# The order of M1 and M2 units in the first chunk of a decoder's MLP

## The chip, the cores and the metric

The kernel runs on one core of a Trainium2 chip. The metric is device time in microseconds (us) of one execution; lower is better.

## What is computed

The reference is a decoder of two layers with 512 tokens and a model width of 1024, in float32. The change lies in the first layer's MLP:

```python
def sq_relu_mlp(h, w1, w2):
    return jnp.square(jax.nn.relu(h @ w1)) @ w2
...
        h = modulate(rmsnorm(x, norm_mlp_g[i]), sh2, sc2)
        x = x + g2[:, None, :] * sq_relu_mlp(h, mlp_w1[i], mlp_w2[i])
```

`w1` is 1024 by 4096 and `w2` 4096 by 1024. Below, M1 is the product with `w1` and M2 the product with `w2`.

## The kernel before

**Precision.** Each float32 operand is split into a high part, rounded to the matmul's input type, and a low part, the rest. A product is three matmuls (function `mm3`, lines 187, 188 and 190): low weight times high operand, high times low, high times high. A weight tile `raw`, `b` or `bt` is split by `split`: ScalarE copies it to `wh` (line 176), then VectorE subtracts to give `wl` (line 177). `parts` does the same to activations (lines 638 and 639). The `wh` and `wl` tiles have five places each.

**The MLP's units.** The 4096 hidden features are worked in four chunks, each of two groups of four 128-feature blocks. The function `mlp` makes a list of units and runs them in order on TensorE, whose order is written out by hand; the compiler orders the other engines. There are four kinds:

- `f`: one 128-feature block of M1 in the plain way (chunk 0 only; the last of them is the first unit of the list).
- `s`, written `(c, j, m)`: one of the seven block products by which M1 for chunk c, group j is formed (a scheme with seven products in place of eight). It has 24 matmuls, each 256 columns wide. Products 1, 6, 7 and 4 accumulate in one PSUM bank and 5, 3 in another, 2 in a third: `start` is set only for m = 1, 5, 2. After products 1, 6 and 5, ScalarE copies the bank to the tile `g` (line 828); after 2, 3 and 7, VectorE combines the bank with `g` (lines 831, 833 and 835); then ScalarE applies relu and square (lines 836 and 667). The next product on a bank may write it only after that read.
- `p`, written `(c, m)`: one of the seven products of M2 for chunk c, 24 matmuls 512 columns wide over two token halves. Products 1, 6, 7 and 4 share one pair of banks, 5 and 3 another. Each is added to `y` on VectorE (line 930; the first time on ScalarE, line 933).
- `q`: the last chunk of M2, in the plain way.

**The weights of a unit.** M1's sums of weight blocks are formed in place. For m = 5 and 6, VectorE adds a block (line 788); after the split of m = 5 and of m = 6, GpSimd issues an accumulating DMA that adds another block for a later product (line 783). Product 4 of a group so uses the tile that product 6 has split, after such a transfer. Plain loads are issued by SyncE (line 159). They share three buffers, and a load waits for a buffer until the last split from it is done. M2's products 1, 5, 6 and 4 go through one tile `bt` in the same way: after each split GpSimd issues the accumulating transfer for the next of them (line 850).

**Preparation ahead.** At each unit n the loop first emits the preparations (loads, sums, splits) of the units from n on that fit a budget: an `s` counts 1, a `p` counts 2, and at most 5 are counted (`ahead`). Then come the extra jobs whose number is n (a modulation column: one-element copy on ScalarE, line 214, and a 128x1024 multiply with accumulation on VectorE, line 215; one column is due at unit 8), and then the run of unit n on TensorE with the reads of its bank.

**The order of units.** For layer 0, chunk 0 the list begins with the rest of `f`; then `lead` units of kind `s`; then, after each `p` in `ORDER2` = (1, 2, 5, 6, 3, 7, 4), as many `s` units as `step` says. The `s` units are those of chunk 1: group 0 in the order 1, 2, 5, 6, 3, 7, 4 and then group 1 in the order 1, 5, 6, 3, 7, 2, 4.

Of the kernel before, what the change touches and what calls it, by code (L numbers as in the profile page):

```python
# [81 lines left out]
def decoder_kernel(ctx: ExitStack, tc: tile.TileContext, xtok, vecs, rows, fgrow, ada0, adag, ada1, pool_w, w1s, w1, w1f, w1b, w2, w2e, w_v, w_u, w_o, wsT, lnp, bs, out):  # L82
# [561 lines left out]
    def mlp(i, first, extra, last, ending):  # L644
# [3 lines left out]
        with (  # L648
# [328 lines left out]
            for c in range(3):  # L977

                early = i == 0 and c == 0
                fs = [("s", (c + 1, j, m)) for j in range(2) for m in (ORDER2 if early and j == 0 else ORDER)]  # L980
                lead, step = (3, (0, 3, 2, 2, 2, 2, 0)) if early else (2, (1, 2, 3, 2, 2, 2, 0))
                units += fs[0:lead]
                fs = fs[lead:]
                for m, n in zip(ORDER2, step):
                    units.append(("p", (c, m)))
                    units += fs[0:n]
                    fs = fs[n:]
# [118 lines left out]
    ex += [(59, lambda: spread_cols(mods[0][:, c_g(1, 0) : c_g(1, 0) + KD], "gain0"))]  # L1106
    ex += [(n, modulation(q, get4)) for q, n in enumerate(COLUMNS) if q >= 19]
    mlp(0, first0, ex, gated, ending0)


# [6 lines left out]
    with (  # L1117
# [79 lines left out]
        for dh in range(2):  # L1197
            wo = blocks(w_o[dh])

            early = 6 if dh == 0 else KD  # L1200
# [60 lines left out]
    ex = [x for q in range(8) for x in modulation_late(48 + q, 8 + 5 * q, late_gb if q == 0 else get_gb)]  # L1261
    ex += [(58, lambda: spread_cols(mods[1][:, c_g(1, 0) : c_g(1, 0) + KD], "gain1"))]
    mlp(1, first1, ex, last1, lambda: None)


# [78 lines left out]
```

## Time and profile before

| what | value |
|---|---|
| three runs | 854.56, 855.83, 855.63 us |
| median | 855.63 us |
| the profiled execution | 853.81 us |
| its span, from first to last instruction | 852.1 us |
| mean granted TensorE clock | 0.993 of full speed |
| moved by DMA | 186.53 MB, 219 GB/s on the mean |

The engines are TensorE (PE; its weight loads are PEld), VectorE (DVE), ScalarE (ACT), GpSimd (POOL) and SyncE (SP). A letter q behind the name is an engine's instruction queue, where DMA issues stand. In a timeline row, the bracket at the end gives the time that the engine stood idle before the instruction and what released it. A matmul's shown length overlaps that of the next: the step from start to start is what one takes from TensorE's time.

The changed stretch lies from about 97 us, when the last `f` unit begins, to 184 us, when chunk 1 begins.

### The profile page before, as it was taken

The page shows a single profiled execution, that of the slowest core. Times are in us where ns is not written, and L with a number is a line of the kernel's source. Part 1 is how long each engine was busy: PE and PEld are TensorE (multiplying, and loading weights), DVE is VectorE, ACT ScalarE, POOL GpSimd, SP SyncE. Part 2 cuts the span into 40 slices and gives each one's busy share as a digit, 9 for nine tenths or more (in the row PEclk, how much of TensorE's full clock was granted, in tenths as well). Part 3 has the DMA queues.
Part 4 walks back from the last instruction along what each step waited for, and adds up shares of the span by engine and source line. Part 5 has one row for each costly group of instructions (what it writes and reads, how often), then busy time and mean ns, then how long its engine had stood idle before and what let it go on. Part 6 is the DMA issues. An engine that isn't in the chain of part 4 may idle for free.

```text
span 852.1 us, 13021 instructions
## 1 busy us (share of the span) xinstructions
PE 837.4 (98%) x5068; PEld 744.6 (87%) x5068; DVE 695.8 (82%) x928; ACT 490.9 (58%) x728; POOL 70.3 (8%) x95
## 2 busy tenths in 40 slices
PE   9999999999999999999999999999999999999996
PEld 7778898998998998888888888999999999999885
DVE  6889798978997998867897865777788888987755
ACT  5286776765756567247233226666766666566521
POOL 3000011010101010000020001010101000111001
PEclk9999999999999999999999999999999999999998
DMA  8969998988888896724745636947888788777302
GB/s 349 418 234 323 357 216 217 288 212 236 211 282 195 274 237 205 272 98 173 256 166 176 218 123 224 320 94 202 208 238 221 207 222 241 182 168 243 125 25 99
DMA packets 44082, 186.53 MB, mean 219 GB/s; under 512 B 4955, under 2 KB 5107, under 8 KB 36726
## 3 DMA queue, kind: packets, MB, share of 16 engines
q1 hardware_dynamic: 35282, 137.72, 43.7%
q0 software_dynamic: 8304, 45.63, 26.7%
q10 hardware_dynamic: 436, 2.37, 0.8%
q8 instruction: 40, 0.66, 0.3%
q14 instruction: 20, 0.16, 0.1%
HBM read 179.39 MB, written 6.30 MB: 218 GB/s over the span
## 4 chain that ended last, share of the span: by engine, by line
PE 87%; DMA 6%; ACT 3%; DVE 2%; issue 1%; SPq 0%; POOLq 0%; POOL 0%; DVEq 0%; ACTq 0%
PE po L187 16%; PE po L188 16%; PE po L190 16%; PE pm L188 12%; PE pm L190 12%; PE pm L187 12%; DMA wh<-in_ada 2%; DMA bt<-in_w 2%; DMA wl<-in_ada 1%; DMA ada<-in_adag 1%; PE po L1182 1%; ACT sq L315 1%; PE px L1062 1%; ACT wh L176 0%; PE po L611 0%
## 5 line engine op out<-in xcount | busy, mean ns | idle before, releaser
L187 PE MATMUL po<-hb,wl 128*128 128x256 f32 (+2 forms) x633 | 187.9, 297 | 2.3 <-ACT g L828 2.1
L188 PE MATMUL po<-hb,wh 128*128 128x256 f32 (+1 forms) x632 | 187.2, 296 | 0.0
L190 PE MATMUL po<-hb,wh 128*128 128x256 f32 (+1 forms) x632 | 187.1, 296 | 0.0
L177 DVE TENSOR_TENSOR wl<-raw,wh 128x1024 fp32r<-128x1024 f32 (+1 forms) x128 | 152.8, 1198 | 39.4 <-ACT wh L176 36.8
L176 ACT ACTIVATE wh<-raw 128x1024 fp32r<-128x1024 f32 (+1 forms) x128 | 131.9, 1038 | 79.6 <-PE pm L190 26.7
L190 PE MATMUL pm<-wh,oh 128*128 128x512 f32 (+1 forms) x375 | 131.1, 367 | 0.0
L187 PE MATMUL pm<-wh,ol 128*128 128x512 f32 x336 | 131.0, 390 | 0.0
L188 PE MATMUL pm<-wl,oh 128*128 128x512 f32 x336 | 131.0, 390 | 0.0
L187 PEld LDWEIGHTS po<-hb,wl 128*128 128x128 f32 x633 | 119.6, 189 | 7.0 <-ACT g L828 2.3
L190 PEld LDWEIGHTS po<-hb,wh 128*128 128x128 f32 x632 | 119.5, 189 | 4.1
L188 PEld LDWEIGHTS po<-hb,wh 128*128 128x128 f32 x632 | 119.4, 189 | 3.9
L190 PEld LDWEIGHTS pm<-wh,oh 128*128 128x128 f32 x375 | 70.4, 188 | 14.7
L187 PE MATMUL po<-as,wl 128*128 128x256 f32 x288 | 79.9, 277 | 0.7 <-DVE wl L177 0.7
L188 PE MATMUL po<-as,wh 128*128 128x256 f32 x288 | 79.6, 277 | 0.0
L190 PE MATMUL po<-as,wh 128*128 128x256 f32 x288 | 79.6, 276 | 0.0
L177 DVE TENSOR_TENSOR wl<-bt,wh 128x1024 fp32r<-128x1024 f32 x48 | 58.4, 1222 | 23.5 <-ACT wh L176 23.5
L215 DVE SCALAR_TENSOR_TENSOR ada<-ada,cb 128x1024 f32<-128x1024 f32 x56 | 68.1, 1219 | 10.4 <-DMA ada<-in_ada 7.8
L187 PEld LDWEIGHTS pm<-wh,ol 128*128 128x128 f32 x336 | 63.1, 188 | 11.9
L188 PEld LDWEIGHTS pm<-wl,oh 128*128 128x128 f32 x336 | 63.1, 188 | 11.7
L176 ACT ACTIVATE wh<-bt 128x1024 fp32r<-128x1024 f32 x48 | 50.3, 1057 | 25.6 <-DMA bt<-in_w 15.9
L187 PEld LDWEIGHTS po<-as,wl 128*128 128x128 f32 x288 | 54.1, 188 | 0.9 <-ACT wh L176 0.9
L188 PEld LDWEIGHTS po<-as,wh 128*128 128x128 f32 x288 | 54.2, 188 | 0.0
(218 smaller groups left out, 1549.9 us busy)
## 6 DMA issues: line engine op xcount, KB each, us to landing
ada<-in_ada SPq DMA_DIRECT2D x72, 512.0 KB, 4.5
raw<-in_w1b SPq DMA_DIRECT2D x48, 512.0 KB, 5.5
b<-in_w SPq DMA_DIRECT2D x18, 1024.0 KB, 6.8
bt<-in_w POOLq DMA_DIRECT2D x18, 1024.0 KB, 8.0
raw<-in_w1b POOLq DMA_DIRECT2D x24, 512.0 KB, 5.7
raw<-in_w2e SPq DMA_DIRECT2D x16, 512.0 KB, 4.3
bt<-in_w SPq DMA_DIRECT2D x6, 1024.0 KB, 9.8
b<-in_w POOLq DMA_DIRECT2D x6, 1024.0 KB, 11.1
```

What stands on the lines that cost most here:

```text
L176: A.activation(h[:, c], r[:, c], AF.Copy)
L177: V.tensor_tensor(l[:, c], r[:, c], f32(h[:, c]), ALU.subtract)
L187: T.matmul(o[:, c], wl, mh[:, c], start=first and not c.start, stop=False, **kw)
L188: T.matmul(o, wh, ml, start=False, stop=False, **kw)
L190: T.matmul(o[:, c], wh, mh[:, c], start=False, stop=last and c.stop is None, **kw)
L215: V.scalar_tensor_tensor(r, r, 1.0, cb, ALU.mult, ALU.mult, accum_out=pmv[i, b][:, j : j + 1])
L315: A.activation(j, X(t)[:, c], AF.Square, scale=D**-0.5, accum_out=out)
L1062: T.transpose(px[:, 256 * q + P * r : 256 * q + P * r + P], xs[r][:, P * (k + q) : P * (k + q) + P], ident)
L1182: T.matmul(po[:, tok[t]], vt[t][:, ch, c0 : c0 + P], wb[:, 0, hd], start=True, stop=True)
```

## The change

One tuple: after product 2 of M2, four `s` units in place of three, and after product 7 one in place of two.

```diff
-                lead, step = (3, (0, 3, 2, 2, 2, 2, 0)) if early else (2, (1, 2, 3, 2, 2, 2, 0))
+                lead, step = (3, (0, 4, 2, 2, 2, 1, 0)) if early else (2, (1, 2, 3, 2, 2, 2, 0))
```

The units with their numbers, S standing for `s` of group 0, T for `s` of group 1, P for `p` of chunk 0:

| n | 5 | 6 | 7 | 8 | 9 | 10 | 11 | 12 | 13 | 14 | 15 | 16 | 17 | 18 | 19 | 20 | 21 |
|---|---|---|---|---|---|---|---|---|---|---|---|---|---|---|---|---|---|
| before | P2 | S6 | S3 | S7 | P5 | S4 | T1 | P6 | T5 | T6 | P3 | T3 | T7 | P7 | T2 | T4 | P4 |
| after | P2 | S6 | S3 | S7 | S4 | P5 | T1 | T5 | P6 | T6 | T3 | P3 | T7 | T2 | P7 | T4 | P4 |

So four M2 units (P5, P6, P3 and P7) each change places with the `s` unit behind them. Units 0 to 8 and 20 onwards keep their numbers, as do the extra jobs. By the budget of `ahead`, the preparations move with them: in the code, P5's goes from unit 6 to unit 7, S4's from 7 to 6, T5's from 10 to 9, P6's from 10 to 11, P3's from 13 to 14, T3's from 13 to 12, P7's from 16 to 17, T2's from 16 to 15, and P4's stays at 19.

## The prediction

> **What bounds the kernel now.** I read the page's shares first, then the list of what TensorE waits for from 98 us to 380 us, then TensorE's timeline around the changed stretch, then ScalarE's and VectorE's timelines of the same microseconds. S1 to S7 are the M1 units of `(1, 0, m)`, T1 to T7 those of `(1, 1, m)`, P1 to P7 the M2 units of chunk 0.
>
> ```profile
> span 852.1 us, 13021 instructions
> PE 837.4 (98%) x5068; PEld 744.6 (87%) x5068; DVE 695.8 (82%) x928; ACT 490.9 (58%) x728; POOL 70.3 (8%) x95
> PE 87%; DMA 6%; ACT 3%; DVE 2%; issue 1%; SPq 0%; POOLq 0%; POOL 0%; DVEq 0%; ACTq 0%
> ```
>
> TensorE is busy 98% of the span and makes 87% of the chain that ended last. So an edit that only reorders TensorE's units (same matmuls, same number) can change the time only through TensorE's idle stretches, and the slow clock behind them. In the stretch of the change there is exactly one:
>
> ```profile
> PE po L187 <- ACT g L828: 2.1, 1, 2.1
> PE po L187 <- DVE wl L177: 0.7, 1, 0.7
> ```
>
> The 2.1 lies here, the 0.7 in chunk 1, at 272 us (last row):
>
> ```profile
> 127.87 0.28 PE L190 MATMUL po<-as,wh 128*128 128x256 f32 x1
> 130.25 0.38 PE L187 MATMUL po<-hb,wl 128*128 128x256 f32 x1 [2.10 <-ACT g L828]
> ...
> 134.58 0.28 PE L190 MATMUL po<-hb,wh 128*128 128x256 f32 x1
> 134.69 0.39 PE L187 MATMUL pm<-wh,ol 128*128 128x512 f32 x1
> ...
> 140.15 0.29 PE L187 MATMUL po<-hb,wl 128*128 128x256 f32 x1
> ...
> 142.89 0.28 PE L187 MATMUL po<-hb,wl 128*128 128x256 f32 x1
> ...
> 145.61 0.39 PE L187 MATMUL pm<-wh,ol 128*128 128x512 f32 x1
> ...
> 272.18 0.36 PE L187 MATMUL po<-as,wl 128*128 128x256 f32 x1 [0.72 <-DVE wl L177]
> ```
>
> Columns: start and length in us, engine, line, operation, tiles, idle time before it and its releaser. The last matmul of S3 starts at 127.87. S7 cannot begin, because it accumulates on the bank that S6's copy (line 828) has still to read. S7 runs from 130.25 to 134.69, P5 to 140.15, S4 to 142.89, T1 to 145.61. S4 and T1 take 5.46 us together, 2.73 each, and P5 takes 5.46. S7 took 4.44, 1.71 more than its sisters. The table by stretch (PE, PEld, DVE, ACT and POOL busy, granted clock, DMA share, GB/s) says why:
>
> ```profile
> 120.00:128.00 8.00, 8.00 (x61) 7.53 (x59) 6.77 (x7) 3.00 (x4) 0.86 (x1) 1.00 1.00 275
> 128.00:130.00 2.00, 0.15 (x2) 0.00 (x0) 1.20 (x2) 2.00 (x3) 0.00 (x0) 1.00 1.04 274
> 130.00:132.00 2.00, 1.75 (x9) 1.76 (x10) 1.16 (x2) 0.47 (x2) 0.55 (x1) 0.63 1.02 385
> 132.00:134.00 2.00, 2.00 (x12) 2.00 (x11) 1.19 (x2) 1.62 (x2) 0.30 (x1) 0.51 1.04 254
> 272.00:274.00 2.00, 1.82 (x16) 1.85 (x17) 2.00 (x4) 2.00 (x3) 0.87 (x1) 1.00 0.84 166
> ```
>
> After the stop of 2.27 us (127.98, one issue step of 0.11 behind 127.87, to 130.25) the granted clock is 0.63 and 0.51; after the one of 0.7 us it stays 1.00. The present stall therefore costs 2.27 + 1.71 = 3.98 us, all that this stretch could give back. The DMA engines are full throughout (share 1.00 to 1.04).
>
> **Why S7 waits, and what stands behind it.** ScalarE, then VectorE, then the descriptor issues of GpSimd and SyncE:
>
> ```profile
> 127.70 2.00 ACT L176 ACTIVATE wh<-bt 128x1024 fp32r<-128x1024 f32 x2 [5.00 <-DMA bt<-in_w]
> 129.62 0.58 ACT L828 ACTIVATE g<-po 128x512 f32<-128x512 f32 x1
> 131.72 1.06 ACT L176 ACTIVATE wh<-raw 128x1024 fp32r<-128x1024 f32 x1 [1.53 <-DMA raw<-in_w1b]
> 133.16 1.06 ACT L176 ACTIVATE wh<-raw 128x1024 fp32r<-128x1024 f32 x1 [0.38 <-DMA raw<-in_w1b]
> 134.25 0.20 ACT L214 ACTIVATE pmv<-wh 128x1 f32<-128x1 f32 x1
> ```
> ```profile
> 132.81 1.23 DVE L177 TENSOR_TENSOR wl<-raw,wh 128x1024 fp32r<-128x1024 f32 x1 [1.65 <-ACT wh L176]
> 133.95 0.69 DVE L833 TENSOR_TENSOR g<-po,g 128x512 f32<-128x512 f32 x1
> 134.55 1.22 DVE L177 TENSOR_TENSOR wl<-raw,wh 128x1024 fp32r<-128x1024 f32 x1
> 135.69 1.22 DVE L215 SCALAR_TENSOR_TENSOR ada<-ada,cb 128x1024 f32<-128x1024 f32 x1
> 136.83 0.68 DVE L835 TENSOR_TENSOR g<-g,po 128x512 f32<-128x512 f32 x1
> ...
> 174.13 1.28 DVE L930 TENSOR_TENSOR y<-y,pm 128x512 f32<-128x512 f32 x2
> ```
> ```profile
> 111.65 0.85 POOL L850 DMA_DIRECT2D bt<-in_w  x1 [0.63 <-DVE wl L177]
> 122.46 0.86 POOL L783 DMA_DIRECT2D raw<-in_w1b  x1 [9.96 <-DVE wl L177]
> 131.45 0.85 POOL L850 DMA_DIRECT2D bt<-in_w  x1 [8.13 <-DVE wl L177]
> ```
>
> P5's two splits stood in ScalarE's queue ahead of S6's copy, and waited until 127.70 for the accumulating transfer issued at 111.65. Next come S4's split (131.72, waiting for its transfer issued at 122.46), T1's (133.16, waiting too) and the one-element copy of line 214. VectorE follows in the order of the code: S4's low part, the combination of S3 (833), T1's low part, the modulation column placed at unit 8 (215), and only then S7's combination (835), done at 136.83 + 0.68 = 137.51.
>
> **The change, part by part.** TensorE goes from S6 S3 S7 P5 S4 T1 P6 T5 T6 P3 T3 T7 P7 T2 T4 P4 to S6 S3 S7 S4 P5 T1 T5 P6 T6 T3 P3 T7 T2 P7 T4 P4. No instruction is added or removed.
>
> *P5 behind S4.* Its preparation moves in the code from unit 6 to unit 7, behind S6's copy; S4's moves ahead from 7 to 6. That can free S7, and is worth 3.98 us at most. The price is that P5's 5.46 us no longer lie between S7 and S4. They cover two things today. First, S4 continues S7's accumulation on the same bank (start only at m = 1, 5, 2), and may not write it before line 835 has read it. Second, S4's weights arrive late: split from 131.72, low part done at 132.81 + 1.23 = 134.04. Both are over by 137.51, 2.64 us ahead of S4's start at 140.15; directly behind S7 they aren't.
>
> When does 835 end then? Everything ahead of it on VectorE stays ahead of it in the code: P5's splits (unit 7 rather than 6), S4's low part (6), 833 (unit 7's run), T1's low part and the column (unit 8), and 835 is unit 8's run. T1's low part hangs on a transfer that lands at 133.1. So I leave 835's end at 137.51, whether S7 runs early or late, and S4 starts 0.05 behind it (as S7 did: 129.62 + 0.58 = 130.20, start 130.25), at 137.56. TensorE has then stood for 2.87 us (from 134.69, S7 still late) or 6.85 (from 127.98 + 2.73 = 130.71, S7 on time). Both are longer than the 2.27 that dropped the clock, so S4 takes 4.44. Sum: 137.56 + 4.44 + 5.46 (P5) = 147.46, against 142.89 where T1 starts now: **+4.57 us**. The bounds of this term: if 835 costs no queueing at all, S4 starts at its own data (134.05), which gives 134.05 + 4.44 + 5.46 = 143.95, +1.06; if S4's data came too, the gain of the last rival below.
>
> In a sentence by itself: the Trainium skill ("TensorE: Matmul & The Clock Gate", "What's actually happening") says that the clock drops after at least one idle window of some 3.4 us, by which 2.87 us of idling could leave S4 at full speed and the sum would be 137.56 + 2.73 + 5.46 - 142.89 = +2.86. The trace disagrees: 2.27 us of idling were followed by a clock of 0.63 and 0.51.
>
> The other three units, with two more rows of TensorE (T5's and T2's first matmul):
>
> ```profile
> 151.07 0.29 PE L187 MATMUL po<-as,wl 128*128 128x256 f32 x1
> ...
> 172.91 0.29 PE L187 MATMUL po<-hb,wl 128*128 128x256 f32 x1
> ```
>
> *P6 behind T5, P3 behind T3.* P6's accumulating issue at 131.45 hangs on P5's split, not on its run, and P6's first matmul (145.61 now) comes 4.57 + 2.73 later, so its transfer gains cover. T5 and T3 each come 5.46 earlier against the M2 unit that they pass. T5 would start at 147.46 + 2.73 = 150.19; it starts at 151.07 now with no wait before it. I take nothing; as nearest row for a loss I take the 0.7 us wait for a low part, below nothing I exclude, since no idle time is left there to win. The orders of the accumulating issues on POOL and of the loads on SP stay (S4's, then P5's; T5's and T6's splits still trigger theirs).
>
> *P7 behind T2.* P4 adds on P7's banks and needs both line-930 adds out of them. P7 ends at 172.91 now, the two adds at 174.13 + 1.28 = 175.41, 2.50 behind it. T4 alone, 2.73, now covers that in place of T2 and T4's 5.46. I take nothing, with 0.23 to spare; another VectorE operation of 1.22 ahead of the adds would cost 1.0.
>
> From T1 on TensorE has no idle time in which a delay could be made up, so +4.57 goes to the end. The profiled execution took 853.81 us (span 852.1 and 1.7 around it), 1.82 below the median of the runs, 855.63. The profiled one becomes 858.4, the median **860.2**.
>
> **The rivals.** One more row, of the page's transfers (the last number is the median of us from issue to landing):
>
> ```profile
> raw<-in_w1b POOLq DMA_DIRECT2D x24, 512.0 KB, 5.7
> ```
>
> *S4's split also goes ahead of S6's copy on ScalarE.* For it: S4's preparation moves to unit 6, ahead of the run of S6. Against: its transfer is issued 10.8 us after P5's, and the compiler places work when it believes it ready. Then the copy follows at 132.78 to 133.3, S7 runs 133.35 to 137.8, P5's splits push T1's to 137.3, and low part, column and 835 end near 140.2. S4 from there, slow, and P5 end at 150.1: +7.2, 862.8.
>
> *835 slips ahead of T1's low part and the column.* For it: the compiler does reorder VectorE when it believes an operand ready. Against: here the rows run in the order of the code. With S7 on time, 835 follows 833 at 134.6 to 135.3, S4 at 135.3, +2.3; with S7 late, 835 ends at 135.5, the stop of 0.9 keeps the clock, S4 at 135.55: +0.9. So 856.5 to 857.9.
>
> *Faster.* S6's copy goes first, S7 runs 127.98 to 130.71, and S4's transfer lands in time. It takes 131.7 - 122.5 = 9.2 us now. The page's median for transfers of this kind is 5.7. With that S4's raw lands at 128.2 and its low part ends near 130.5; 835 alone stands between S7 and S4, some 0.8 us, too short to drop the clock: 3.98 - 0.8 = 3.2 gained, 852.4. It decides from S4's start: to gain anything, this must come before 142.89 - 5.46 - 2.73 = 134.70 with the clock kept, and before 132.99 with the clock dropped, and 835 must stand at the head of VectorE's queue as well. Against it: a DMA share of 1.00 to 1.04 until 134 us, with the same transfers ahead, which makes S4's data end at 134.04.
>
> *The clock holds* through S4's stop of 2.87. The rows show it kept after 0.72 and dropped after 2.27, once each, and a single drop may have had its moment by chance. S4 then takes 2.73: 137.56 + 2.73 + 5.46 = 145.75, +2.86, 858.5. Against it stands the 0.51. (The window of the Trainium skill's page is a reason for it.)
>
> **How the numbers follow.** Forecast 0.50; S4's split ahead of the copy 0.12; 835 early 0.18; faster 0.14; clock holds 0.06. What a measurement here tells from no change is about 0.2%, 1.71 us. Faster beyond that: most of the faster case, 0.11. Within: half of 835 early and the rest of the faster case, 0.12. Slower: 0.50 + 0.12 + 0.09 + 0.06 = 0.77. The range begins at 855.0, where most of the faster case is left out, and ends at 863.4, the second case plus half of the 1.0 at P7; outside lies some 0.15.
>
> **What would show it.** Right: in the profile after, S4's first matmul shows an idle time of 2.5 us or more released by VectorE's line 835, with the clock near 0.5 for 3 us behind it, and 835 stands behind T1's low part and line 215. S7's wait for line 828 may be gone or not; it doesn't change the sum. Wrong: S4 waits for line 177 (its own data decide), or for under 1 us; or TensorE stops in front of P4; or S7 waits longer than now.

## The result, and the profile after

| kernel | runs | median, us | lowest to highest |
|---|---|---|---|
| before | 6 | 855.25 | 853.51 to 857.06 |
| changed | 6 | 863.29 | 859.18 to 865.73 |

The ratio is 1.0092, with a 95% interval of 1.0065 to 1.0119: the changed kernel is slower by 8.0 us. The profiled execution is the slowest of its six (865.73 us), so its stretches are read against each other rather than its span.

The shares of the page and the list of TensorE's waits after the change:

```profile
span 863.7 us, 13019 instructions
PE 845.0 (98%) x5068; PEld 750.5 (87%) x5068; DVE 696.8 (81%) x928; ACT 492.0 (57%) x728; POOL 69.8 (8%) x95
PE 75%; DVE 9%; DMA 8%; ACT 4%; issue 4%; POOLq 0%; DVEq 0%; POOL 0%; ACTq 0%
```
```profile
PE po L187 <- ACT g L828: 4.7, 1, 4.7
PE po L187 <- DVE g L835: 3.0, 1, 3.0
...
PE pm L187 <- DVE y L930: 0.6, 1, 0.6
```

TensorE's part of the chain that ended last fell from 87% to 75%, and VectorE's rose from 2% to 9%. The forecast let the stall on S6's copy (line 828) go or stay; it more than doubled. A second one, on S7's combination (line 835), came new, as forecast. TensorE's rows there are S7's, S4's, P5's and T1's first matmul:

```profile
133.31 0.57 PE L187 MATMUL po<-hb,wl 128*128 128x256 f32 x1 [4.71 <-ACT g L828]
...
140.96 0.58 PE L187 MATMUL po<-hb,wl 128*128 128x256 f32 x1 [3.04 <-DVE g L835]
...
146.25 0.63 PE L187 MATMUL pm<-wh,ol 128*128 128x512 f32 x1
...
152.09 0.29 PE L187 MATMUL po<-hb,wl 128*128 128x256 f32 x1
```

T1 starts at 152.09 in place of 142.89, 9.20 later. S6 began at 122.98 in place of 122.53 here, so the stretch from S6 to T1 takes 29.11 us in place of 20.36, 8.75 more. Why S7 waited so long stands in ScalarE's rows, and why S4 did in VectorE's:

```profile
122.13 1.04 ACT L638 ACTIVATE oh<-s 128x1024 fp32r<-128x1024 f32 x1
131.71 1.06 ACT L176 ACTIVATE wh<-raw 128x1024 fp32r<-128x1024 f32 x1 [8.54 <-DMA raw<-in_w1b]
132.67 0.58 ACT L828 ACTIVATE g<-po 128x512 f32<-128x512 f32 x1
133.15 1.99 ACT L176 ACTIVATE wh<-bt 128x1024 fp32r<-128x1024 f32 x2
135.05 1.04 ACT L176 ACTIVATE wh<-raw 128x1024 fp32r<-128x1024 f32 x1
```
```profile
132.80 1.23 DVE L177 TENSOR_TENSOR wl<-raw,wh 128x1024 fp32r<-128x1024 f32 x1 [5.56 <-ACT wh L176]
133.94 1.22 DVE L869 TENSOR_TENSOR s<-s,g 128x1024 f32<-128x1024 f32 x1
135.07 2.35 DVE L177 TENSOR_TENSOR wl<-bt,wh 128x1024 fp32r<-128x1024 f32 x2
137.34 0.69 DVE L833 TENSOR_TENSOR g<-po,g 128x512 f32<-128x512 f32 x1
137.94 1.22 DVE L177 TENSOR_TENSOR wl<-raw,wh 128x1024 fp32r<-128x1024 f32 x1
139.08 1.22 DVE L215 SCALAR_TENSOR_TENSOR ada<-ada,cb 128x1024 f32<-128x1024 f32 x1
...
140.22 0.68 DVE L835 TENSOR_TENSOR g<-g,po 128x512 f32<-128x512 f32 x1
```

ScalarE took S4's split first and stood 8.54 us for its transfer, with S6's copy behind it; P5's two splits, whose data had landed by 127.70 in the kernel before, followed the copy. On VectorE, P5's low parts then stood behind S4's and ahead of 833, T1's low part, the column and 835, and so did line 869, which forms P6's operand. In the kernel before, P5's low parts had run ahead of S4's, and line 869 behind 835:

```profile
128.80 2.36 DVE L177 TENSOR_TENSOR wl<-bt,wh 128x1024 fp32r<-128x1024 f32 x2 [2.02 <-ACT wh L176]
...
137.50 1.22 DVE L869 TENSOR_TENSOR s<-s,g 128x1024 f32<-128x1024 f32 x1
```

S4's low part started when it had started before (132.80 and 132.81), and from there VectorE worked without a gap. From start to start, line 869 took 1.13 us and P5's two low parts 2.27. Their sum is what 835's end moved, from 137.51 to 140.90. The granted clock (the third number from the end, after five engines' busy times; then DMA share and GB/s) dropped behind both stops:

```profile
134.00:136.00 2.00, 2.00 (x11) 2.00 (x11) 2.00 (x3) 2.00 (x4) 0.00 (x0) 0.50 0.46 143
136.00:138.00 2.00, 1.91 (x14) 1.72 (x12) 2.00 (x4) 1.13 (x3) 0.28 (x1) 0.81 0.30 119
...
140.00:142.00 2.00, 1.04 (x5) 1.04 (x6) 2.00 (x5) 1.03 (x2) 0.00 (x0) 0.54 1.02 205
142.00:144.00 2.00, 2.00 (x11) 2.00 (x11) 1.95 (x3) 1.26 (x2) 0.86 (x1) 0.50 0.94 197
...
146.00:148.00 2.00, 2.00 (x10) 1.67 (x9) 0.00 (x0) 1.51 (x3) 0.00 (x0) 0.75 1.02 209
```

### The profile page after: what moved, and what is told of

It is laid out like the page before. It is cut to its first block, busy times and chain, and to the rows that moved or that the text cites. A ratio compares the mean times of both kernels' runs of the same rounds, so it can differ in the third digit from the quotient of the medians.

```text
span 863.7 us, 13019 instructions
## 1 busy us (share of the span) xinstructions
PE 845.0 (98%) x5068; PEld 750.5 (87%) x5068; DVE 696.8 (81%) x928; ACT 492.0 (57%) x728; POOL 69.8 (8%) x95
## 4 chain that ended last, share of the span: by engine, by line
PE 75%; DVE 9%; DMA 8%; ACT 4%; issue 4%; POOLq 0%; DVEq 0%; POOL 0%; ACTq 0%
PE po L187 13%; PE po L190 13%; PE po L188 13%; PE pm L187 9%; PE pm L188 9%; PE pm L190 9%; DVE wl L177 4%; DMA raw<-in_w1b 4%; DMA ada<-in_ada 3%; PE po L479 2%; PE pg L431 1%; ACT wh L176 1%; DVE ada L215 1%; DMA bt<-in_w 1%; DVE y L930 1%
## 5 line engine op out<-in xcount | busy, mean ns | idle before, releaser
L187 PE MATMUL po<-hb,wl 128*128 128x256 f32 (+2 forms) x633 | 189.8, 300 | 7.9 <-ACT g L828 4.7
L188 PEld LDWEIGHTS po<-hb,wh 128*128 128x128 f32 x632 | 121.1, 192 | 3.9
L190 PEld LDWEIGHTS po<-hb,wh 128*128 128x128 f32 x632 | 120.5, 191 | 4.1
```

The costliest lines, as they stand in the source:

```text
L187: T.matmul(o[:, c], wl, mh[:, c], start=first and not c.start, stop=False, **kw)
L188: T.matmul(o, wh, ml, start=False, stop=False, **kw)
L190: T.matmul(o[:, c], wh, mh[:, c], start=False, stop=last and c.stop is None, **kw)
```

## The experiments

Ratios are to the kernel before, run on the same chip with each.

**Which of the four swaps costs.** The change taken apart: P5 behind S4 alone, and the other three units alone.

```diff
-(0, 3, 2, 2, 2, 2, 0)
+(0, 4, 1, 2, 2, 2, 0)    p5_alone
+(0, 3, 3, 2, 2, 1, 0)    others_alone
```

> Only P5 and S4 change places; T5, T6, T3, T7, T2 stand as before against P6, P3 and P7. Theory A (the loss sits in front of S7 and S4, from P5's move alone): 863.3, within 1.5, with two idle times of TensorE of about 4.7 and 3.0 us, released by lines 828 and 835. Rival C (a part of the loss comes from the other three units): clearly under 863, down to 860 if half of it lies there.

> P5 stays ahead of S4; P6, P3 and P7 move behind T5, T3 and T2. Theory A: no change, 855.3 within 1.7, with S7's idle time of 2.1 us on line 828 as before and no new one in chunk 0. Rival C: 857 to 859, with a new idle time in front of P4 or one of the moved units.

`p5_alone` took 863.61 us, ratio 1.0092 (1.0069 to 1.0115), as much as the whole change, with the same two waits:

```profile
PE po L187 <- ACT g L828: 4.6, 1, 4.6
PE po L187 <- DVE g L835: 3.0, 1, 3.0
```

`others_alone` took 856.45 us, ratio 1.0029 (1.0012 to 1.0045): a miss for "no change". S7's wait was 0.7 us there, not the expected 2.1, and P4 waited for P7's adds. TensorE's row comes first, then VectorE's:

```profile
177.78 0.47 PE L187 MATMUL pm<-wh,ol 128*128 128x512 f32 x1 [1.41 <-DVE y L930]
```
```profile
175.81 1.23 DVE L177 TENSOR_TENSOR wl<-raw,wh 128x1024 fp32r<-128x1024 f32 x1 [1.18 <-ACT wh L176]
176.95 1.27 DVE L930 TENSOR_TENSOR y<-y,pm 128x512 f32<-128x512 f32 x2
```

A low part stood ahead of the adds and waited for ScalarE. To see whether P7 makes that price, P6 and P3 were moved without it, by `(0, 3, 3, 2, 1, 2, 0)`.

> P6 and P3 move behind T5 and T3, P5 and P7 stay as before. In the run others_alone (856.45 against 854.06) P4 waited 1.4 us for the line-930 adds of P7. Theory G (that wait is the price of the three units, as P7's shorter cover): no wait in front of P4, 854.1 within 1.0. Rival C' (T5 and T3 ahead of P6 and P3 cost it): 856.4 again.

It took 856.17 us, ratio 1.0004 (0.998 to 1.0028), with no wait in front of P4. S7, in the same place in both runs, waited 0.7 us there and 2.9 here. The missing wait at P4 fits P7's shorter cover as the price, but the two intervals overlap, so it isn't shown. In the profile of the whole change P4 doesn't wait, so this price isn't always paid there.

**The state that the forecast had assumed.** The changed order on TensorE, with S4's preparation behind P5's, so that ScalarE and VectorE keep the order of before as far as T1's split.

```diff
-                for m in range(n, ahead(n)):
+                for m in {6: (6, 7, 8), 7: (7, 8, 10, 9)}.get(n if i == 0 else None, range(n, ahead(n))):
```

> TensorE's order of the changed kernel, but S4's preparation is put behind P5's at unit 7, so that ScalarE and VectorE keep the order of the kernel before up to T1's split. This is the state that the forecast assumed. The forecast's step: S7 waits 2.1 us on line 828 as before, 835 ends at 137.5 and S4 starts there: 855.25 + 4.6 = 859.8. Theory A (S4's split ahead of the copy on ScalarE adds the rest): the same 859.8, and so 3.4 of the 8.0 us come from that queue. Rival D (P5's missing cover alone costs all of it, whatever ScalarE's order): 863.3.

It took 859.84 us, ratio 1.0063 (1.0038 to 1.0087). S4 started at 137.58, where the forecast had put it (137.56), and the release is the forecast's. S7's wait was 1.2 us rather than 2.1:

```profile
129.68 0.38 PE L187 MATMUL po<-hb,wl 128*128 128x256 f32 x1 [1.20 <-ACT g L828]
...
137.58 0.58 PE L187 MATMUL po<-hb,wl 128*128 128x256 f32 x1 [4.81 <-DVE g L835]
...
142.87 0.44 PE L187 MATMUL pm<-wh,ol 128*128 128x512 f32 x1
```

`p5_alone`, run beside it, has a median 3.8 us higher. So about that much of the loss goes with ScalarE's order and what it does to VectorE's; the two intervals overlap, so the size is rough. The edit put P5's low parts back ahead of S4's and line 869 back behind 835 (138.65) at once, and can't part those two. Rival D's 863.3 lies outside the interval.

**Does S7's start matter?** The same kernel, with S6's copy on VectorE, where it goes ahead of P5's low parts.

```diff
-                    A.activation(t, po, AF.Copy)
+                    V.tensor_copy(t, po) if (i, c, j, m) == (0, 1, 0, 6) else A.activation(t, po, AF.Copy)
```

> The kernel of the run after_s4_behind with S6's copy on VectorE, ahead of P5's low parts, so that S7 doesn't wait at all. The forecast said that whether S7 runs early or late doesn't change the sum. Theory A: S7 starts at 128 us, TensorE then stands for 6.8 us until line 835 ends, S4 starts at 137.5 as in after_s4_behind, and the time is 1.0063 of the kernel before, within 0.0025. Rival I (an earlier S7 is worth something): 1.0045 or less, with S4 at 135.5 or earlier.

It took 859.9 us, ratio 1.007 (1.0042 to 1.0097). S7 started on time, at 128.22; S4 waited 6.45 us and began at the same moment as in `after_s4_behind`:

```profile
137.56 0.58 PE L187 MATMUL po<-hb,wl 128*128 128x256 f32 x1 [6.45 <-DVE g L835]
```

So in this order 835 decides when S4 starts, and S7's start doesn't.

**What decides 835.** First VectorE's queue: T1's preparation and the column one unit later, on top of `after_s4_behind`.

```diff
+... 8: (8, 9, 10)} ...
-COLUMNS = (0, 5, 8, 11, ...
+COLUMNS = (0, 5, 9, 11, ...
```

> The kernel of the run after_s4_behind, and T1's preparation at unit 9 and the modulation column due at unit 9 in place of 8, so that line 835 (S7's combination) no longer stands behind T1's low part or line 215 on VectorE. Theory A (S4 waits for 835, and 835 for what is queued ahead of it): 835 ends some 1.2 to 2.3 us earlier, S4 starts at 135.3 to 136.4 in place of 137.6, and the time is 857.5 to 858.7 against 859.84. Rival E (VectorE is full here, and what moves behind 835 is missed in front of P5 or T5): 859.8 again, with a new idle time there.

It took 857.77 us, ratio 1.0035 (1.0014 to 1.0056). VectorE's rows show that only the column moved behind 835; T1's low part still stood ahead of it:

```profile
134.04 1.22 DVE L177 TENSOR_TENSOR wl<-raw,wh 128x1024 fp32r<-128x1024 f32 x1
135.17 0.68 DVE L835 TENSOR_TENSOR g<-g,po 128x512 f32<-128x512 f32 x1
```

S4 started at 135.91, 1.67 earlier than in `after_s4_behind`. The column makes 1.13 of that; the rest is that S4's low part began at 132.30 in place of 132.83, with its transfer landing earlier. No new wait appeared in front of P5 or T5. The median is 2.1 us below that of `after_s4_behind`, as expected, but the two ran on different chips, and the intervals of their ratios overlap. Rival E's 859.8 against 854.06 would be 1.0067, outside this run's interval. The next run takes the transfer away. It leaves one block out of S4's weight sum, so it only probes the time:

```diff
-                if m == 6:
+                if m == 6 and (i, c, j) != (0, 1, 0):
                     add(t, *CHAIN[4])
```

> The changed kernel without the accumulating transfer into S4's weights (product 4 of chunk 1, group 0, layer 0 is computed with its weight sum one block short). S4's split waits for nothing then. Theory A (both stops of the changed kernel come from that transfer's landing at 131.7, by ScalarE's queue): S7's wait shrinks from 4.7 to about 1.2 us (P5's first split still stands ahead of the copy), 835 ends at 135.5 to 137.5 behind T1's split, and the time is 856.8 to 858.8 against 854.1 before. Rival F (all the loss is that transfer's): 854 or less. Rival D (P5's missing cover): 862 to 863.

It took 855.87 us, ratio 1.0014 (0.9995 to 1.0033): less than theory A had asked. S7 didn't wait; T1's transfer, with 512 KB less on the way, landed at 129.19, in place of 133.16 in the kernel before; and 835 let S4 go at 134.18:

```profile
129.19 1.06 ACT L176 ACTIVATE wh<-raw 128x1024 fp32r<-128x1024 f32 x1 [0.93 <-DMA raw<-in_w1b]
```
```profile
134.18 0.58 PE L187 MATMUL po<-hb,wl 128*128 128x256 f32 x1 [2.84 <-DVE g L835]
```

From S6 to T1 it took 22.30 us, against 20.36 before and 29.11 after the change. So most of the loss hangs on what lands when, by S4's transfer itself and by its share of full DMA engines; the run can't part these two. The missing cover still costs: S4 stood 2.84 us and then took 5.28, and the stall of S7 that is gone here pays for only a part of that.

**What the old stall was worth.** The kernel before, with S6's copy on VectorE and P5's preparation at unit 7.

```diff
-                for m in range(n, ahead(n)):
+                for m in range(n, 9 if (i, n) == (0, 6) else ahead(n)):
```

> The kernel before with S6's copy on VectorE, ahead of P5's low parts there, so that S7 no longer hangs on ScalarE's wait for P5's transfer. If the stall in front of S7 is worth the 2.27 us and the slow clock behind it: 855.25 - 3.9 = 851.3, no idle time in front of S7 and a clock of 1.00 from 128 to 136 us. Rival: the next late item takes its place (P5's own low part, ready at 131.1 against 130.7): P5 waits 0.4 us, 851.7. If the stall was worth only its idle time: 853.0.

It took 856.15 us, ratio 1.0012 (0.9997 to 1.0028). That is a miss: nothing was gained. The wait on line 828 is gone from TensorE's list, the clock stays 1.00, and others stand in its place:

```profile
PE pm L187 <- DVE ol L639: 1.3, 1, 1.3
PE pm L187 <- DVE y L930: 1.2, 1, 1.2
...
PE po L187 <- DVE g L835: 1.0, 1, 1.0
```

S4 can't start before 835 in the old order either (137.50 here), P6 waits for its operand at 144.73, and in chunk 1 a unit waits for line-930 adds. With 835 ahead of the column a part of it comes:

```diff
-                for m in range(n, 9 if (i, n) == (0, 6) else ahead(n)):
+                for m in range(n, {6: 9, 8: 11}.get(n if i == 0 else None, ahead(n))):
-COLUMNS = (0, 5, 8, 11, ...
+COLUMNS = (0, 5, 9, 11, ...
```

> The kernel of the run before_copy_vector, and T1's preparation and the modulation column at unit 9. There S4 waited 1.0 us for line 835, and P6 1.3 us for the low part of its operand. Theory H (S7's stop is only the first of several things that end at the same time, set by the transfers): S4's wait goes, P6's stays or grows by the same, 853 to 855.5 against 854.06. Rival (the first stop is all that counted): 851.0 to 852.

It took 853.3 us, ratio 0.9976 (0.9958 to 0.9995). The same kernel ran once more:

> The kernel of the run before_read_early again, beside the one with the operand formed early: 0.9976 of the kernel before, between 0.9955 and 0.9995. Theory H: no wait for S7 and S4, one of about 1 us in front of P6.

It took 853.12 us, ratio 0.9978 (0.9963 to 0.9993). In this run S7 and S4 wait no longer; P6 does, and a unit in chunk 1:

```profile
142.84 0.50 PE L187 MATMUL pm<-wh,ol 128*128 128x512 f32 x1 [0.71 <-DVE ol L639]
...
206.71 0.47 PE L187 MATMUL pm<-wh,ol 128*128 128x512 f32 x1 [0.78 <-DVE y L930]
```

This is the one version here that is faster than the kernel before, by some 2 us. Going after P6's wait as well, by forming its operand early (line 869 behind P5's operand split), gained nothing further:

```diff
                 parts((oh, ol), a)
+                if (i, c, m) == (0, 0, 5):
+                    V.tensor_tensor(a, a, quad(c, 0, 0), ALU.subtract)
```

> The kernel of the run before_read_early, in which only P6 still waited (0.95 us for the low part of its operand), with the subtraction that forms this operand (line 869) emitted behind P5's operand split rather than at P6's preparation. Theory H: P6's wait goes or gives way to one for P6's weights, ready 0.2 to 0.4 us before that low part: 0.2 to 0.9 us below the run before_read_early_2 of the same call.

It took 854.23 us, ratio 0.9993 (0.9973 to 1.0012), 1.1 us more than `before_read_early_2` beside it. P6 then waited 0.6 and 0.8 us for its weights, and the wait in chunk 1 grew to 1.4.

## Why the prediction was right, and where not

**The direction and its cause were right.** Without P5 between them, S4 waits for 835, and 835 for VectorE's queue. The signs that the forecast had named for this came: TensorE stood 3.04 us in front of S4 for line 835, which had T1's low part and line 215 ahead of it, and the clock was 0.54 and 0.50 behind the stop. Where ScalarE kept the old order, S4's start (137.58 and 137.56, forecast 137.56) and release came out as worked out. P5's swap alone gave the ratio of the whole change (1.0092).

**The size was wrong, and the range held by luck.** The forecast was +4.57, the medians moved by 8.0. The 863.29 lies inside the stated range by 0.1 us only, and the range reached that far because the first rival's 862.8 and half of a price at P7 set its end. One of the forecast's own signs of being wrong came too: S7 waited longer than before (4.71 against 2.10). In the profile the parts add up: 4.57 as forecast, 3.40 for S4's later start (140.96 against 137.56) and 1.23 more for the clock, less the 0.45 by which S6 began later, make the 8.75.

**The step that failed** is "I leave 835's end at 137.51, whether S7 runs early or late", on the ground that "Everything ahead of it on VectorE stays ahead of it in the code". That S7's start doesn't matter held (`after_s7_on_time`). But 835 ended at 140.90. S4's split ran ahead of S6's copy on ScalarE, as its preparation now stands in the code, and waited until 131.71 for its transfer. So P5's splits came at 133.15 in place of 127.70, and P5's low parts (2.27) behind S4's on VectorE, not ahead of it. And line 869 (1.13), which the forecast's list doesn't have, came ahead of 835; what it costs by itself is open, as no run moves it alone. T1's split, at 135.05 in place of 133.16, added nothing here: it was done at 136.09, before VectorE came to T1's low part at 137.94. With the old order back on both engines (`after_s4_behind`), 835 ended at 137.53.

This was the first rival, given 0.12 against 0.50 for the forecast. The evidence put against it, that S4's transfer is issued 10.8 us after P5's, tells when the data land and not in which order the compiler queues the work. The rival had the copy and S7's start right (132.67 and 133.31, against 132.78 and 133.35). It had 835 end near 140.2 because T1's split was to be pushed to 137.3, which didn't happen; other work, P5's low parts and line 869, took about as long. So that its +7.2 comes close to the 8.0 is in part luck.

**The clock's term** had a price that one profile can't fix. S4 was given 4.44 us at the dropped clock, as S7 took before. It took 5.29 in the changed kernel, where P5 took 5.84 in place of 5.46; together that is the 1.23 above. It took 5.29 in `after_s4_behind` too, where the stretch grew by 5.17 in place of 4.57, but 4.17 in `p5_alone`.

**The worth of the old stall** was mis-sized: 3.98 us were called "all that this stretch could give back". The stall cost 2.27 and a slow clock where it stood. But behind it lay only 2.64 us of slack in S4's start, and P6 could start only 0.9 earlier with the stall gone (144.73 in place of 145.61); the waits came up there (`before_copy_vector`). The "faster" rival rested on the same worth. What the stretch gave in the end was some 2 us, in the version that moved 835 too.

**P7 behind T2** was taken at nothing, with 1.0 us if one more operation stood ahead of the adds. With the three units alone that came about: a low part stood ahead of them, and P4 waited 1.41. That this wait is all of that run's 0.3% isn't shown.

**That the clock might hold** through a stop of 2.87 us was the rival with 0.06. It fell: S4's idle times of 2.84 (`after_no_add`), 3.04 and 4.81 us were followed by 0.50.

## What to carry to other kernels

A unit that stands between two others on the busiest engine is cover for what the second needs. Before moving it, list everything that this unit hides, and on the other engines ask which waiting instruction the new order puts at the head of their queues, not only which ones stay ahead of which; and look for work that can come in between, as line 869 did. A stall that the profile shows need not be worth its length: look how much slack the next two or three units have, for here the same late transfers set their starts too.

## What the runs showed of the hardware

The clock's price for a stop varied, and not with the stop's length. A stop of 1.4 us (`after_s4_behind`, S7: idle 1.20) left the clock at 1.00; S7 took 2.92 there, 0.19 more than the usual 2.73. The one of 2.27 us in the kernel before cost 1.71. The longer ones in front of S4:

| run | TensorE idle before S4, us | S4 took, us |
|---|---|---|
| `after_no_add` | 2.84 | 5.28 |
| `p5_alone` | 3.03 | 4.17 |
| changed kernel | 3.04 | 5.29 |
| `after_read_early` | 4.42 | 4.46 |
| `after_s4_behind` | 4.81 | 5.29 |
| `after_s7_on_time` | 6.45 | 4.83 |

After the same stop (3.03 and 3.04) the clock was back at 1.00 some 3 us behind S4's start in `p5_alone`, whose rows follow, and after some 6 us in the changed kernel:

```profile
142.00:144.00 2.00, 2.00 (x12) 2.00 (x11) 2.00 (x3) 0.27 (x1) 0.42 (x1) 0.53 1.06 221
144.00:146.00 2.00, 2.00 (x16) 1.87 (x15) 0.42 (x1) 0.00 (x0) 0.44 (x1) 1.00 0.94 283
```

So the same stop cost 1.5 us more in one of these two kernels than in the other. Whether executions of one program differ in this way, and whether that makes the spread of the changed kernel's runs (859.18 to 865.73), wasn't tried. The Trainium skill ("TensorE: Matmul & The Clock Gate", "What's actually happening") says that the clock drops after at least one idle window of some 3.4 us, in a window that runs free of the program. The wandering length would fit a free-running window; the drop after the stop of 2.27 us doesn't fit the 3.4 us.
